# Scores of 64 rows in the two row halves of TensorE: time mixing head by head, sparse attention two parities at a time

## The chip, the cores and the metric

One core of one Trainium2 chip. The metric is the device time of one launch in microseconds (us), the median of several runs. The engines are PE (TensorE), with its weight loads shown apart as PEld, DVE (VectorE), ACT (ScalarE), POOL (GpSimd) and SP (SyncE, which issues DMAs). PSUM has eight banks of 128 x 512 in f32.

## What is computed

Two transformer blocks after one another on a row of 256 tokens of 1024 values, in f32. Each has two mixers and two feed-forward layers. The change is in three of the mixers: RWKV time mixing, differential attention and sparse attention. Cut to what matters:

```python
# time mixing, 16 heads of 64: a state S per head, token by token
sa = einsum('bhvk,bhk->bhv', S, a)
S = S * w[:, :, None, :] + sa[..., None] * b[:, :, None, :] + v[..., None] * k[:, :, None, :]
y = einsum('bhvk,bhk->bhv', S, r)
...
# differential attention, 8 heads with two scores (c) of 64 each
s = einsum('bqhcd,bkhcd->bhcqk', qb, k)
p = softmax(where(mask, s, -inf))
a = p[:, :, 0] - lam * p[:, :, 1]
...
# sparse attention: 64 keys of each query chosen by 8 index heads, then 16 heads of 64
dots = einsum('bqhe,bke->bqhk', qib, k_idx)
score = einsum('bqh,bqhk->bqk', wb, relu(dots))
vals, idx = top_k(where(mask, score, -inf), topk)
s = einsum('bqhd,bqkhd->bhqk', qb, gather(k, idx))
```

## The kernel before

The stages run in the order time mixing, ffn, latent attention, ffn, differential attention, mlp, sparse attention, mlp. Tokens are two blocks (b) of 128. The large products take three matmuls each, of high and low parts of both sides (L284, L285, L286, 128 x 512 per matmul or 128 x 256); L88 on ACT and L89 on DVE or POOL cut each weight tile into its parts when it has come by DMA.

A stage puts its latency-bound steps (generators) and the large products (a list `bg`, stepped by `tick`) into one program order; `weave` steps the generators in turn, `attention` runs `part1` (scores, softmax) of each item and `part2` (transposed rows times V) `lag` items later, with so many ticks behind each. The final order on each engine is not this one: the tile framework's scheduler sets it from priorities (attention's steps carry one) and its own timeline. On the chip each engine then runs its row in that order, and waits by semaphores.

The scores have 64 rows to contract. Features lie two heads to a tile of 128 partitions, so head s of a pair is the half 64s to 64s + 63. In the attentions a head's score is a matmul of K = 64 in one half (L1137, L1287 for the index heads, L1311). In time mixing `rwkv_scores` takes both heads of a pair in one matmul of K = 128: its right side is a tile of 256 columns in which each head's 128 columns have zeros in the other head's rows (L1820, two pairs to a bank, then the mask L1822 on DVE and a yield; twice per call). It is called 16 times: by block and half of the features (H) for the system matrix (`rwkv_strict`), V's part (`rwkv_solve`), and two reads (`rwkv_reads`). After the first of these come, in time mixing:

- L1717: 32 x 32 blocks of the system on PE, their mask L1719, splits L1725 to L1729, and a transpose L1728;
- L1735 to L1746: forward substitution on DVE, 14 rounds of a product (L1740) and a sum (L1741), closed by L1744 to L1746;
- `rwkv_merge`: L1763, L1770, L1783, L1796, small products of 16 and 32 columns on PE with DVE steps between, for each half;
- `rwkv_solve` (L1835, L1838, L1846, L1851) and `rwkv_out` (L1935, L1938, L1942), matmuls of 64 columns.

PSUM is split in rings by kind: time mixing takes its scores from a ring `tp` of four banks (four more are for products or longer sums, by part), the attentions from one of three. `turns` gives the SBUF rooms that `take` hands out: e for softmax rows, n and o for smaller ones, r for the relu rows of `select`, which finds the 64 keys by eight rounds of DVE (L1302, L1303).

Of the kernel before, what the change touches and what calls it, by code (L numbers as in the profile page):

```python
# [15 lines left out]
AF = mybir.ActivationFunctionType  # L16
# [3 lines left out]
T = 256  # L20
# [9 lines left out]
class Feeder:  # L30
    """Weights in the order of their use: DMA ahead, then cut into two float32r parts, in tiles that go round."""
# [14 lines left out]
    def grow(self, n):  # L46
        """Slots for n more units cut ahead; those that are too many go as they get free."""
# [53 lines left out]
    def put(self, unit):  # L101
        """The unit has had its last use."""
        self._give(unit[2])
# [33 lines left out]
def first(f):  # L137
    """The method's instructions go before others that are ready, those of block 0 before those of block 1."""
# [10 lines left out]
class K:  # L149
# [20 lines left out]
    def turns(self, **n):  # L170
        """Slots for one kind of tile each, taken in turn, till the next call."""
# [11 lines left out]
    def rings(self, acc=4, tp=4, long=0, po=0):  # L183
        """The banks of PSUM in rings: products, short-lived, longer-lived, halves for attention's sums."""
# [17 lines left out]
    def sm(self, n, tag=None, bufs=None):  # L202
        """A few columns, taken in turn from as many as there are of that kind."""
# [9 lines left out]
    def wide(self, key, n, bufs):  # L213
        """The same for wider ones."""
# [7 lines left out]
    def bcast(self, vec, n, q=None):  # L222
        """A row of DRAM on every partition, in a slot."""
# [17 lines left out]
    def sumsq(self, parts, n):  # L241
        """Mean of squares of the rows over n columns, from the parts of a row; [128, len(parts)]."""
# [9 lines left out]
    def rstd(self, ss, eps=EPS):  # L252
        """(sum of the columns of ss + eps) ** -0.5"""
# [9 lines left out]
    def transpose_split(self, src, hi, lo, b, kts):  # L263
        """Token-major columns of src (128 each) to feature-major parts of block b."""
# [27 lines left out]
    def gemm_b_steps(self, nkt, widths, lhs, done, rk=2, tail=0, head=0, before_b1=None):  # L292
        """Token-major products: for each column piece, acc[b][128 tokens, width]; yields after each weight unit."""
# [51 lines left out]
    def gemm_b1(self, nkt, nh, lhs, done, rk=2):  # L345
        """Token-major products, all columns of block 0 before block 1: the weights are kept between."""
# [33 lines left out]
    def weave(self, gens, every=1, n=1):  # L380
        """One step of each in turn; n steps of the products behind them after every so many turns."""
# [24 lines left out]
    def pre_norm(self, b, g):  # L406
        """x * rstd * g of block b, token-major."""
# [15 lines left out]
    def norm_in(self, g):  # L423
        """The normed rows of both blocks, feature-major, before the weights that had to wait."""
# [6 lines left out]
    class PostNorm:  # L431
        """x += m * rstd(m) * g, the columns of m arriving in halves."""
# [18 lines left out]
    class Add:  # L451
        """x += m"""
# [10 lines left out]
    def load_rows_t(self, pieces, name):  # L463
        """Rows of 128 values (a vector cut in rows, several vectors under one another) as columns."""
# [24 lines left out]
    def gemm_a(self, hi, lo):  # L489
        """Feature-major product: two tiles of 128 features, 256 tokens."""  # L490
# [14 lines left out]
    def gemm_a_first(self, hi, lo):  # L505
        """Two such products, of the blocks one after the other: token-major, then turned."""
# [118 lines left out]
    def rope_setup(self):  # L625
        """cos and sin of [token, block, frequency]: 16 of the first block's, 8 of the second's."""
# [40 lines left out]
    def rope_pair(self, x1, x2, cos1, sin1, cos2, sin2, room=None):  # L667
        """x1, x2 <- x1 cos1 - x2 sin1, x2 cos2 + x1 sin2 (all [128, heads, half])."""
# [1374 lines left out]
```

## Time and profile before

| | us |
|---|---|
| median of 3 runs | 1434.3 |
| lowest and highest | 1432.52 and 1442.06 |
| profiled execution, span | 1429.5 |
| PE busy | 1351.8 |
| DVE busy | 937.9 |
| ACT busy | 705.4 |

The profiled execution is shown by its span, from the first to the last instruction; the time of a run has a few us around it. A matmul in f32 is two records of PE in the trace, one in the cut parts. An entry such as 64*128 64x256 says that the tile mode is 64 rows by 128 columns of the array and that 64 partitions with 256 columns move. PE pipelines, so the time from one start to the next says what a matmul takes of it, and its length is longer.

### The profile page before, as it was taken

The numbers are of one execution on the slowest core, as the hardware profiler recorded it, in microseconds if no ns is written. First come the engines' busy times: TensorE is split into PE (matmuls) and PEld (weight loads), VectorE is DVE, ScalarE is ACT, GpSimd is POOL, SyncE is SP. The second block draws the span as 40 slices with busy tenths as digits, with TensorE's granted clock in tenths as the row PEclk, the third lists the DMA queues.
The fourth block names the chain that finished last, engine by engine and source line by source line (L and its number), as shares of the span: only waits on it lengthen the run. The fifth ranks groups of instructions, "written<-read, shape, count | busy, mean of one in ns | idle before, by whom it ended". The sixth has DMA issues, their size and how long they took to land. (4 is left out here: it accounts for less than half of the span.)

```text
span 1429.5 us, 22837 instructions
## 1 busy us (share of the span) xinstructions
PE 1351.8 (95%) x8907; PEld 1178.2 (82%) x8907; DVE 937.9 (66%) x1526; ACT 705.4 (49%) x1168; POOL 370.7 (26%) x300
## 2 busy tenths in 40 slices
PE   7978799999999899999999999999999998999998
PEld 5667699799988787799987777699888777799987
DVE  7899755777654775767644788667433896576542
ACT  5753222565543665565553555455443546465431
POOL 6545841200000100132232353222322531111110
PEclk9989699999999999999999999999999999999999
DMA  7323301475573452366574543266663642266562
GB/s 245 118 88 120 102 4 61 161 228 185 184 235 99 148 166 59 96 218 192 187 213 135 177 148 118 89 197 202 210 192 97 206 121 72 74 193 191 191 193 88
DMA packets 153420, 214.39 MB, mean 150 GB/s; under 512 B 11668, under 2 KB 95868, under 8 KB 153312
## 3 DMA queue, kind: packets, MB, share of 16 engines
q1 hardware_dynamic: 152448, 209.78, 47.1%
q10 hardware_dynamic: 864, 3.15, 0.6%
q8 instruction: 70, 1.15, 0.3%
q14 instruction: 38, 0.31, 0.1%
HBM read 211.85 MB, written 1.05 MB: 149 GB/s over the span
## 5 line engine op out<-in xcount | busy, mean ns | idle before, releaser
L88 ACT ACTIVATE s_slot<-s_slot 128x1024 fp32r<-128x1024 f32 (+2 forms) x221 | 229.4, 1048 | 178.4 <-PE bank L286 95.1
L89 DVE TENSOR_TENSOR s_slot<-s_slot,s_slot 128x1024 fp32r<-128x1024 f32 (+3 forms) x172 | 221.5, 1296 | 132.2 <-ACT s_slot L88 130.8
L89 DVE TENSOR_TENSOR rwkv_slot<-s_slot,rwkv_slot 128x1024 fp32r<-128x1024 f32 (+4 forms) x121 | 157.4, 1309 | 119.1 <-ACT rwkv_slot L88 118.7
L89 POOL TENSOR_TENSOR s_slot<-s_slot,s_slot 128x1024 fp32r<-128x1024 f32 x49 | 119.3, 2437 | 310.3 <-ACT s_slot L88 295.7
L88 ACT ACTIVATE rwkv_slot<-s_slot 128x1024 fp32r<-128x1024 f32 (+3 forms) x141 | 144.2, 1035 | 106.2 <-PE bank L286 64.1
L260 POOL TENSOR_TENSOR rwkv_sm<-rwkv_sm,mhalf 128x1 f32<-128x1 f32 x32 | 20.0, 625 | 338.0 <-DVE rwkv_sm L257 337.2
L284 PE MATMUL bank<-ffn_slot,s_slot 128*128 128x256 f32 x320 | 90.8, 284 | 2.4 <-DVE ffn_slot L539 2.4
L285 PE MATMUL bank<-ffn_slot,s_slot 128*128 128x256 f32 x320 | 90.6, 283 | 0.0
L286 PE MATMUL bank<-ffn_slot,s_slot 128*128 128x256 f32 x320 | 90.6, 283 | 0.0
L284 PE MATMUL bank<-ffn_slot,rwkv_slot 128*128 128x256 f32 x280 | 79.4, 284 | 0.0
L285 PE MATMUL bank<-ffn_slot,rwkv_slot 128*128 128x256 f32 x280 | 79.3, 283 | 0.0
L286 PE MATMUL bank<-ffn_slot,rwkv_slot 128*128 128x256 f32 x280 | 79.2, 283 | 0.0
L284 PE MATMUL bank<-mlp_slot,s_slot 128*128 128x256 f32 x272 | 77.0, 283 | 0.0
L286 PE MATMUL bank<-mlp_slot,s_slot 128*128 128x256 f32 x272 | 77.0, 283 | 0.0
L285 PE MATMUL bank<-mlp_slot,s_slot 128*128 128x256 f32 x272 | 77.0, 283 | 0.0
L89 POOL TENSOR_TENSOR rwkv_slot<-s_slot,rwkv_slot 128x1024 fp32r<-128x1024 f32 (+1 forms) x20 | 48.3, 2413 | 93.6 <-ACT rwkv_slot L88 89.6
L284 PEld LDWEIGHTS bank<-ffn_slot,s_slot 128*128 128x128 f32 x320 | 61.4, 192 | 2.8 <-ACT rwkv_slot L88 1.4
L284 PE MATMUL bank<-s_slot,mlp_slot 128*128 128x512 f32 x160 | 62.6, 391 | 0.4 <-ACT mlp_slot L274 0.3
L286 PE MATMUL bank<-s_slot,mlp_slot 128*128 128x512 f32 x160 | 62.6, 391 | 0.0
L285 PE MATMUL bank<-s_slot,mlp_slot 128*128 128x512 f32 x160 | 62.3, 389 | 0.0
L286 PEld LDWEIGHTS bank<-ffn_slot,s_slot 128*128 128x128 f32 x320 | 61.4, 192 | 0.0
L285 PEld LDWEIGHTS bank<-ffn_slot,s_slot 128*128 128x128 f32 x320 | 61.4, 192 | 0.0
(516 smaller groups left out, 3917.7 us busy)
## 6 DMA issues: line engine op xcount, KB each, us to landing
s_slot<-in_mlp_w_dram SPq DMA_DIRECT2D x128, 512.0 KB
s_slot<-in_ffn_w_in_dram SPq DMA_DIRECT2D x88, 512.0 KB
s_slot<-in_ffn_w_out_dram SPq DMA_DIRECT2D x44, 512.0 KB
s_slot<-in_a_w_rkv_dram SPq DMA_DIRECT2D x24, 512.0 KB
s_slot<-in_diff_w_in_dram SPq DMA_DIRECT2D x32, 256.0 KB
s_slot<-in_dsa_w_in_dram SPq DMA_DIRECT2D x16, 512.0 KB
s_slot<-in_a_w_o_dram SPq DMA_DIRECT2D x8, 512.0 KB
s_slot<-in_o_w_dram SPq DMA_DIRECT2D x8, 512.0 KB
```

The lines of the kernel that those rows point to most:

```text
L88: k.nc.scalar.activation(hi, raw, AF.Copy)
L89: (k.nc.gpsimd if low else k.nc.vector).tensor_tensor(lo, raw, hi, op=OP.subtract)
L260: nc.gpsimd.tensor_tensor(r, u, self.mhalf[:, 0:1], op=OP.pow)
L284: mm(out, lh, rh, start=start, stop=False)
L285: mm(out, lh, rl, start=False, stop=False)
L286: mm(out, ll, rh, start=False, stop=stop)
```

## The change

Four places. `rwkv_scores` takes two banks, one for each row half, and makes one matmul of K = 64 per head, alternating between the halves; the masks follow per bank (a strided view of S), with one yield. Differential attention takes its two banks first and alternates between them. `select` does the same with its two halves, and takes its relu rooms from e. `attend` gets tuples of parities: sparse attention takes both parities of a group in one item, with a lag of 1 instead of 3, ticks [4, 2, 2, 2] instead of [2, 1, 1, 1] and rooms e = 6 without r; latent attention keeps one parity per item. Lines behind these move: L1717 is L1727, L1735 to L1741 are L1745 to L1751, L1746 is L1756, L1820 is L1832, L1822 is L1834, L1835 is L1847, L1851 is L1863, L1935 is L1947, L1942 is L1954, L1311 is L1321.

```diff
-    def attend(self, score, V, scale, sel, out, ready, ticks, lag, order):
+    def attend(self, score, V, scale, sel, out, ready, ticks, lag, order, both):
...
-            pr = (4 * g + s, 4 * g + 2 + s)
-            ps = self.tp()
-            for i, hd in enumerate(pr):
-                score(hd, b, ps[:, i * 256:i * 256 + nk], nk)
-            e = self.take("e", 2, 2, 256)
+            ps = [self.tp() for _ in ss]
             for i in range(2):
+                for s, p in zip(ss, ps):
+                    score(4 * g + 2 * i + s, b, p[:, i * 256:i * 256 + nk], nk)
+            es = [self.take("e", 2, 2, 256) for _ in ss]
...
-        self.attention([[(*i, s) for i in items for s in range(2)] for items in self.items(order)], part1, part2, ready, ticks, lag)
+        parts = [(0, 1)] if both else [(0,), (1,)]
+        self.attention([[(*i, ss) for i in items for ss in parts] for items in self.items(order)], part1, part2, ready,
+                       ticks, lag)
...
-            for c in range(2):
-                ps = self.tp()
-                for i in range(2):
+            pss = [self.tp() for _ in range(2)]
+            for i in range(2):
+                for c, ps in enumerate(pss):
                     nc.tensor.matmul(ps[:, i * 256:i * 256 + nk], QK.head(g, 2 * i + c, b * 128, b * 128 + 128),
                                      QK.head(g, 4 + 2 * i + c, 0, nk), start=True, stop=True)
+            for c, ps in enumerate(pss):
...
-        self.turns(e=5, n=4, o=2, r=2)
+        self.turns(e=6, n=4, o=2)
...
-            for j, (i, s) in enumerate(((0, 0), (0, 1), (1, 0), (1, 1))):
-                ps = self.tp()
-                rows = slice(64 * s, 64 * s + 64)
-                rl = self.take("r", 2, 256)
+            for i in range(2):
+                pss = [self.tp() for _ in range(2)]
                 for m in range(2):
-                    nc.tensor.matmul(ps[:, m * 256:m * 256 + nk], IQ[rows, 2 * i + m, b * 128:(b + 1) * 128],
-                                     IK[rows, 0, :nk], start=True, stop=True)
...
+                    for s, ps in enumerate(pss):
+                        rows = slice(64 * s, 64 * s + 64)
+                        nc.tensor.matmul(ps[:, m * 256:m * 256 + nk], IQ[rows, 2 * i + m, b * 128:(b + 1) * 128],
+                                         IK[rows, 0, :nk], start=True, stop=True)
+                rls = [self.take("e", 2, 256) for _ in range(2)]
...
-                    ready, [2,1,1,1], 3, 1)
+                    ready, [4,2,2,2], 1, 1, True)
...
         S = self.slot([128, 8, 128])
-        for j in range(2):
-            p = self.tp()
-            for i in range(2):
-                nc.tensor.matmul(p[:, 256 * i:256 * i + 256], F[:, 2 * j + i, tok], rhs[:, 2 * j + i], start=True,
-                                 stop=True)
-            nc.vector.tensor_tensor(S[:, 4 * j:4 * j + 4], p.rearrange("p (m t) -> p m t", m=4),
+        Sv = S.rearrange("p (f s) t -> p s f t", s=2)
+        ps = [self.tp() for _ in range(2)]
+        for f in range(4):
+            for s, p in enumerate(ps):
+                r = slice(64 * s, 64 * s + 64)
+                nc.tensor.matmul(p[:, 128 * f:128 * f + 128], F[r, f, tok], rhs[r, f, s], start=True, stop=True)
+        for s, p in enumerate(ps):
+            nc.vector.tensor_tensor(Sv[:, s], p.rearrange("p (m t) -> p m t", m=4),
                                     self.over_heads(self.tri[kind], 4), op=OP.mult)
-            yield
+        yield
         return S
```

The order of the instructions moves with it. On PE in the late part of time mixing, before (L1820 the scores, L1935 the reads times V; banks 67 to 70 are the scores'):

```order
L1820 MATMUL bank_67<-rwkv_slot_1565,rwkv_slot_622 128x256
L1820 MATMUL bank_68<-rwkv_slot_1574,rwkv_slot_635 128x256
L1820 MATMUL bank_69<-rwkv_slot_1530,rwkv_slot_725 128x256
L1820 MATMUL bank_70<-rwkv_slot_1540,rwkv_slot_736 128x256
L1820 MATMUL bank_68<-rwkv_slot_1574,rwkv_slot_635 128x256
L1820 MATMUL bank_69<-rwkv_slot_1530,rwkv_slot_725 128x256
L1820 MATMUL bank_67<-rwkv_slot_1565,rwkv_slot_622 128x256
L1935 MATMUL bank_71<-rwkv_slot_325,rwkv_slot_1751 128x64
L1935 MATMUL bank_72<-rwkv_slot_326,rwkv_slot_1759 128x64
L1935 MATMUL bank_71<-rwkv_slot_325,rwkv_slot_1751 128x64
```

The same place after (L1832 the scores, one head each, each bank with one half; L1947 the former L1935):

```order
L1832 MATMUL bank_69<-rwkv_slot_1560,rwkv_slot_725 128x128
L1832 MATMUL bank_67<-rwkv_slot_1618,rwkv_slot_635 128x128
L1832 MATMUL bank_68<-rwkv_slot_1570,rwkv_slot_635 128x128
L1947 MATMUL bank_71<-rwkv_slot_325,rwkv_slot_1782 128x64
L1832 MATMUL bank_70<-rwkv_slot_1609,rwkv_slot_622 128x128
L1832 MATMUL bank_69<-rwkv_slot_1560,rwkv_slot_725 128x128
L1947 MATMUL bank_71<-rwkv_slot_325,rwkv_slot_1782 128x64
L1832 MATMUL bank_67<-rwkv_slot_1618,rwkv_slot_635 128x128
L1832 MATMUL bank_70<-rwkv_slot_1609,rwkv_slot_622 128x128
L1947 MATMUL bank_71<-rwkv_slot_325,rwkv_slot_1782 128x64
L1832 MATMUL bank_68<-rwkv_slot_1570,rwkv_slot_635 128x128
L1832 MATMUL bank_67<-rwkv_slot_1618,rwkv_slot_635 128x128
```

Scores that stood in a row of eight now stand one to three at a time between calls of 64 columns.

On DVE at the head of the forward substitution, before (L1725, L1726, L1728 make its operand, L1822 are masks of scores, L1735 and L1740 its first steps):

```order
L1725 TENSOR_SCALAR rwkv_slot_786<-rwkv_slot_783,even_odd 128x32x16
L1822 TENSOR_TENSOR rwkv_slot_843<-bank_71,rwkv_slot_266 128x512
L1726 SCALAR_TENSOR_TENSOR rwkv_slot_786<-rwkv_slot_783,even_odd,rwkv_slot_786 128x32x16
L1728 STREAM_TRANSPOSE rwkv_slot_785<-rwkv_slot_786 128x512
L1822 TENSOR_TENSOR rwkv_slot_931<-bank_72,rwkv_slot_266 128x512
L1822 TENSOR_TENSOR rwkv_slot_935<-bank_73,rwkv_slot_266 128x512
L1735 COPY rwkv_slot_785<-rwkv_slot_785 128x2
L1822 TENSOR_TENSOR rwkv_slot_931<-bank_74,rwkv_slot_266 128x512
L1822 TENSOR_TENSOR rwkv_slot_935<-bank_71,rwkv_slot_266 128x512
L1740 TENSOR_TENSOR rwkv_slot_787<-rwkv_slot_785 128x2x4
```

The same place after (L1735, L1736, L1738 make the operand, L1834 are the masks, L1745 and L1750 the first steps):

```order
L1739 TENSOR_SCALAR rwkv_slot_784<-rwkv_slot_783,even_odd 128x32x16
L1834 TENSOR_TENSOR rwkv_slot_919<-bank_72,rwkv_slot_266 128x4x128
L1834 TENSOR_TENSOR rwkv_slot_930<-bank_74,rwkv_slot_266 128x4x128
L1735 TENSOR_SCALAR rwkv_slot_786<-rwkv_slot_783,even_odd 128x32x16
L1834 TENSOR_TENSOR rwkv_slot_930<-bank_71,rwkv_slot_266 128x4x128
L1834 TENSOR_TENSOR rwkv_slot_919<-bank_73,rwkv_slot_266 128x4x128
L1736 SCALAR_TENSOR_TENSOR rwkv_slot_786<-rwkv_slot_783,even_odd,rwkv_slot_786 128x32x16
L1738 STREAM_TRANSPOSE rwkv_slot_785<-rwkv_slot_786 128x512
L1745 COPY rwkv_slot_785<-rwkv_slot_785 128x2
L1750 TENSOR_TENSOR rwkv_slot_787<-rwkv_slot_785 128x2x4
```

The masks of the same four banks of scores (slots 931 and 935 before, 919 and 930 after) stand behind L1728 before, and ahead of L1736 after.

On PE, the scores for which these masks wait, after (bank_72 and bank_74, bank_71 and bank_73 are the masks' banks in turn; L284 to L286 large products):

```order
L286 MATMUL bank_69<-s_slot_85,rwkv_slot_863 128x512
L1832 MATMUL bank_71<-rwkv_slot_204,rwkv_slot_736 128x128
L284 MATMUL bank_69<-s_slot_85,rwkv_slot_861 128x512
L285 MATMUL bank_69<-s_slot_86,rwkv_slot_861 128x512
L1832 MATMUL bank_71<-rwkv_slot_204,rwkv_slot_736 128x128
L286 MATMUL bank_69<-s_slot_85,rwkv_slot_863 128x512
L284 MATMUL bank_70<-s_slot_85,rwkv_slot_861 128x512
L1832 MATMUL bank_74<-rwkv_slot_204,rwkv_slot_736 128x128
L1832 MATMUL bank_72<-rwkv_slot_192,rwkv_slot_725 128x128
L1832 MATMUL bank_71<-rwkv_slot_204,rwkv_slot_736 128x128
L285 MATMUL bank_70<-s_slot_86,rwkv_slot_861 128x512
L1832 MATMUL bank_73<-rwkv_slot_192,rwkv_slot_725 128x128
```

Before, these scores (L1820 on banks 71 to 74) were two rows of calls with products between the rows; after, the last ones stand singly between products.

## Rows read from the trace of the kernel before

**Rows 1.** Part 1 of the page: busy time, share of the span and instructions of each engine.

```profile
PE 1351.8 (95%) x8907; PEld 1178.2 (82%) x8907; DVE 937.9 (66%) x1526; ACT 705.4 (49%) x1168; POOL 370.7 (26%) x300
```

**Rows 2.** Table by stretches; columns: length, busy PE, PEld, DVE, ACT, POOL, PEclk, DMA share, GB/s.

```profile
105.00:143.00 38.00, 32.90 (x268) 26.95 (x266) 35.00 (x54) 15.59 (x20) 18.57 (x10) 0.96 0.40 125
143.00:182.00 39.00, 31.40 (x827) 26.39 (x828) 29.18 (x32) 10.37 (x16) 32.52 (x19) 0.64 0.31 93
182.00:245.00 63.00, 62.77 (x562) 58.86 (x561) 31.00 (x58) 10.49 (x19) 15.82 (x37) 1.00 0.08 26
...
1165.00:1200.00 35.00, 29.71 (x144) 22.50 (x142) 30.23 (x100) 19.34 (x52) 10.43 (x8) 0.90 0.30 91
```

**Rows 3.** Timeline of PE, the merge; columns: start, length, engine, line, operation, idle before.

```profile
148.05 1.22 PE L1820 MATMUL bank<-rwkv_slot,rwkv_slot 128*128 128x256 f32 x2
...
153.04 2.37 PE L1770 MATMUL bank<-rwkv_slot,rwkv_slot 32*32 32x16 f32 x204
...
185.64 1.89 PE L1820 MATMUL bank<-rwkv_slot,rwkv_slot 128*128 128x256 f32 x8
187.47 0.73 PE L1851 MATMUL bank<-rwkv_slot,rwkv_slot 64*64 64x64 f32 x9
```

**Rows 4.** Timeline of PE: a burst in both halves, and a burst in one.

```profile
1141.23 1.13 PE L1287 MATMUL bank<-dsa_slot,dsa_slot 64*128 64x256 f32 x8
1142.29 0.50 PE L286 MATMUL bank<-s_slot,dsa_slot 128*128 128x512 f32 x1
...
878.50 0.40 PE L286 MATMUL bank<-rwkv_slot,diff_slot 128*128 128x512 f32 x1
878.83 1.13 PE L1137 MATMUL bank<-diff_slot 64*128 64x256 f32 x4
879.88 0.50 PE L284 MATMUL bank<-rwkv_slot,diff_slot 128*128 128x512 f32 x1
880.22 0.39 PE L285 MATMUL bank<-rwkv_slot,diff_slot 128*128 128x512 f32 x1
```

**Rows 5.** Timeline of PE: single calls in one half between transposes.

```profile
861.98 0.48 PE L1137 MATMUL bank<-diff_slot 64*128 64x128 f32 x2
862.39 0.33 PE L268 MATMUL bank<-ident,diff_slot 128*128 128x128 f32 x1
862.65 0.48 PE L1137 MATMUL bank<-diff_slot 64*128 64x128 f32 x2
```

**Rows 6.** Waits of PE, 143 to 182 us: total, times, longest.

```profile
PE bank L1763 <- DVE rwkv_slot L1744: 5.1, 1, 5.1
PE bank L1770 <- issue: 3.0, 1, 3.0
```

**Rows 7.** Timeline of PE and DVE around the forward substitution.

```profile
107.85 2.06 PE L1717 MATMUL bank<-rwkv_slot,rwkv_slot 128*32 128x64 f32 x128
...
115.99 1.12 DVE L1726 SCALAR_TENSOR_TENSOR rwkv_slot<-rwkv_slot,even_odd,rwkv_slot 128x512 f32<-128x512 f32 x1
...
120.22 0.15 DVE L1740 TENSOR_TENSOR rwkv_slot<-rwkv_slot 128x8 f32<-128x8 f32 x1
...
121.69 2.04 DVE L1740 TENSOR_TENSOR rwkv_slot<-rwkv_slot 128x50 f32<-128x50 f32 x1
...
124.07 2.29 DVE L1740 TENSOR_TENSOR rwkv_slot<-rwkv_slot 128x72 f32<-128x72 f32 x1
...
143.44 0.71 DVE L1746 STREAM_TRANSPOSE rwkv_slot<-rwkv_slot 128x512 f32<-128x512 f32 x1
```

**Rows 8.** Timeline of POOL and ACT in the same stretch.

```profile
121.25 2.40 POOL L89 TENSOR_TENSOR s_slot<-s_slot,s_slot 128x1024 fp32r<-128x1024 f32 x1 [2.19 <-issue]
...
122.73 1.06 ACT L88 ACTIVATE s_slot<-s_slot 128x1024 fp32r<-128x1024 f32 x1 [1.61 <-PE bank L286]
```

**Rows 9.** Sparse attention's scores, grouped (min/median/max ns, first and last start), and PE's wait.

```profile
L1311 PE MATMUL bank<-dsa_slot,dsa_slot x64: 272/374/480, 1164.6 to 1225.9; 64*128 64x128 f32 x32, 64*128 64x256 f32 x32
...
1185.64 0.69 PE L717 MATMUL bank<-ident,dsa_slot 128*128 128x128 f32 x2 [1.68 <-DVE dsa_slot L1054]
```

More of the change, by code (lines that the diff above doesn't have):

```diff
@@ L773, in part1, with part2 @@
         def part1(it):
-            g, b, s = it
+            g, b, ss = it
             nk = 128 * (b + 1)
-            if s == 0:
+            if ss[0] == 0:
                 po[g, b], sums[g, b] = self.bank("po"), self.sm(4, tag="sums", bufs=4)
-            pr = (4 * g + s, 4 * g + 2 + s)
-            ps = self.tp()
-            for i, hd in enumerate(pr):
-                score(hd, b, ps[:, i * 256:i * 256 + nk], nk)
-            e = self.take("e", 2, 2, 256)
-            self.soft_rows(ps, nk, scale, sel and sel[b], [sums[g, b][:, hd % 4:hd % 4 + 1] for hd in pr], e[:, 0], e[:, 1])
-            return e
-        def part2(it, e):
-            g, b, s = it
-            t = self.p_transpose([e[:, 0, 0], e[:, 0, 1]], b + 1, e[:, 1])
-            for i in range(2):
-                hd = 4 * g + 2 * i + s
-                for kb in range(b + 1):
-                    nc.tensor.matmul(po[g, b][:, hd % 4 * 64:hd % 4 * 64 + 64], t[:, i, kb, :], V(kb, hd), start=kb == 0,
-                                     stop=kb == b)
-            if s == 0:
+            ps = [self.tp() for _ in ss]
+            for i in range(2):
+                for s, p in zip(ss, ps):
+                    score(4 * g + 2 * i + s, b, p[:, i * 256:i * 256 + nk], nk)
+            es = [self.take("e", 2, 2, 256) for _ in ss]
+            for s, p, e in zip(ss, ps, es):
+                self.soft_rows(p, nk, scale, sel and sel[b], [sums[g, b][:, 2 * i + s:2 * i + s + 1] for i in range(2)],
+                               e[:, 0], e[:, 1])
+            return es
+        def part2(it, es):
+            g, b, ss = it
+            for s, e in zip(ss, es):
+                t = self.p_transpose([e[:, 0, 0], e[:, 0, 1]], b + 1, e[:, 1])
+                for i in range(2):
+                    hd = 4 * g + 2 * i + s
+                    for kb in range(b + 1):
+                        nc.tensor.matmul(po[g, b][:, hd % 4 * 64:hd % 4 * 64 + 64], t[:, i, kb, :], V(kb, hd),
+                                         start=kb == 0, stop=kb == b)
+            if ss[-1] == 0:
                 return None
@@ L1281, in select @@
             sc, wk, md = box[:, 0, :nk], box[:, 1, :nk], box[:, 2, :nk]
[L1282 to L1285 removed]
+            for i in range(2):
+                pss = [self.tp() for _ in range(2)]
                 for m in range(2):
[L1287 to L1296 removed]
+                    for s, ps in enumerate(pss):
[3 more added lines that the diff above has]
+                rls = [self.take("e", 2, 256) for _ in range(2)]
+                for ps, rl in zip(pss, rls):
+                    nc.scalar.activation(rl[:, :, :nk], ps.rearrange("p (m k) -> p m k", m=2)[:, :, :nk], AF.Relu)
+                for s, rl in enumerate(rls):
+                    for m in range(2):
+                        hd = 2 * (2 * i + m) + s
+                        w = wi[b][:, hd:hd + 1]
+                        if i == s == m == 0:
+                            nc.vector.tensor_scalar(sc, rl[:, 0, :nk], w, None, op0=OP.mult)
+                        else:
+                            nc.vector.scalar_tensor_tensor(sc, rl[:, m, :nk], w, sc, op0=OP.mult, op1=OP.add)
                 yield
```

10 lines of the change are left out of this document (1 added, 9 removed).

## Prediction

> **What bounds the kernel now.** I read the page's busy shares first: PE is busy for 95% of the span, so it is the engine to look at [rows 1]. Then the table by stretches [rows 2]: from 182 to 245 us PE has 62.77 us of work in 63, so what is added to PE there or taken away moves the end one for one. From 105 to 143 it has 32.90 of 38, from 143 to 182 31.40 of 39 at a clock of 0.64: there a chain on DVE and the short products that follow it hold the time. From 1165 to 1200 DVE's search for the 64 largest scores and PE share the time (30.23 and 29.71 of 35). In the feed-forward stages nothing is changed but, here and there, the order of products; I take ±1 us for them.
>
> The profiled span is 1429.5 us, the median of the runs 1434.3; the 4.8 us between lie around the program, and I take them as constant. The runs lie 9.5 us apart, so about 1% (14 us) is what a measurement can tell from no change.
>
> **Prices.** Each matmul in f32 is two records. From the starts on PE: eight records of L1820 (128 x 256) take 187.47 - 185.64 = 1.83 us, the change of mode behind them in it [rows 3], so 0.216 each for those inside the row; one of 64 x 256 has as many columns and is taken alike, one of 64 x 128 at half, 0.11 (two of them and the step out of them are 0.41 [rows 5]). Two bursts in different row halves with different banks do run side by side where they stand next to each other: 8 records of L1287 (four of 128 columns in one half, four of 256 in the other) take from their start to the next 1142.29 - 1141.23 = 1.06 us, and four of 64 x 256 alone 879.88 - 878.83 = 1.05 [rows 4]. So the halves are worth what the change says, if the order lets them meet.
>
> What a burst in row halves costs beside its records is in the same stretches: the first record after the change of mode comes 0.33 us after an f32r product that takes 0.23 otherwise, and the product behind it 0.34 [rows 4]. With 4 x 0.216 = 0.86 of work in the 1.05, one trip into the halves and out costs 0.10 + 0.19 + 0.11 = 0.40 us. Between transposes of one record, 861.98 to 862.65 is one round with three records of 0.11 in 0.67 us: 0.34 per trip [rows 5]. A lone head there pays 0.34 for 0.22 of work. Each change of mode shows in each of these rows, so I count every one.
>
> The Trainium skill's page "TensorEngine Tiling (Array Packing)", section "Key Properties", says that changing the tiling mode, and not only the tile, drains TensorE. The rows agree (0.34 to 0.40 a trip), and the page gives no price. Its section "Theoretical Speedup" promises up to two times for 64 rows; by that the scores would take half as long, which is rival (c).
>
> **The change part by part.**
>
> *Time mixing, late part (from 187 us on).* Here PE is full. Before, the scores are K = 128 calls in the same mode as the products around them, in rows of eight; in the order after, single heads alternate with single calls of L1947, the former L1935. Counted over the whole order from the first L1851 to the first L1942: 9 changes of mode before, 61 after, so 26 trips more. At 0.34 that is +8.8 us (at 0.29, if part of the first record's delay is hidden, 7.5; at 0.40, 10.4). Against it the work: 72 records of 0.216 before are 15.6 us; after, 80 heads are 160 records of 0.112, 17.9 us one after the other, and 13.1 with those halves side by side that the order puts next to each other: -2.5 us. Sum **+6.3 us**, from +5 to +8. The masks stay 32 of the same size.
>
> *Time mixing, early part (107 to 187 us).* Three things. First PE's work: 56 records of 0.216 (12.1 us) become 48 heads in 10.8 us one by one, or 6.2 as the order pairs them; the changes of mode go from 10 to 24, 7 trips or 2.4 to 2.8 us. So PE does some 3 us less, in a stretch in which it waited 5.1 us for L1744 and 3.0 within the merge anyway [rows 6].
>
> Second, DVE's queue. The forward substitution (L1740 and L1741, 14 rounds) starts at 120.22 and its last transpose at 143.44 [rows 7]. In the order after, the four masks of the second scores stand ahead of L1736 and L1738, which feed the chain's head (before: behind L1728). The first of them, of bank_72, waits for a single head that stands on PE behind two bursts of heads, 15 + 5 products of L284 to L286 and three other singles. From the start of L1717 (107.85 [rows 7], L1727 after): 2.2 us for L1727, 4.8 for 26 heads in three visits, 20 products at 0.23 with 0.34 for the first of a row, 5.0, and 4 singles at 0.34 + 0.22 with some of them paired, 1.7: about 121.5, where DVE with its four earlier masks would be ready at about 115. Behind it come the other three masks, L1735, L1736, L1738 and L1745; now the same steps without the first splitting one (0.5) take 120.22 - 115.99 = 4.2 us [rows 7], so the chain's first round would start at about 126, **some 6 us later**. Queued behind are all rounds of the chain, and PE's L1763 waits for its end. Against that, rounds of L1740 last 2.04 and 2.29 us where the first takes 0.15 [rows 7], beside an L89 on POOL of 2.40 us [rows 8]; each L89 follows an L88 on ACT that waits for PE's L286 [rows 8], not for the chain, so one or two would be done before the late head begins. That gives back 1.9 to 3.9 us, and a third such round may follow; I take 3.5, so the chain ends about 3 us later.
>
> Third, the merge (143 to 187 us) after the chain. Before, PE puts L1820 and products between L1763, L1770, L1783, L1796 and L1851: 5.0 us from 148.05 to 153.04, and again before L1851 begins at 187.47 [rows 3]. After, 8 heads and 5 products of these stand ahead of the merge. Part of them is cover for the waits (PE idles 3.0 for L1770 beside them [rows 6]); the first filler alone is 5.0 us, and if that much was in the way, the end of the merge comes 5 us sooner, from 2 to 8. Sum for the early part **-2 us**, from -6 to +7.
>
> *Sparse attention.* The 32 calls of L1311 are 32 records of 0.112 and 32 of 0.216, 10.5 us [rows 9]. Two banks stand next to each other in one place before and in four after, three of them in different halves: 10.05 us of work becomes 8.74, and three trips go, at 0.40: -2.5. In the selection the order splits the pairs that met before (1141.23 is one [rows 4]): 5 bursts become 7 and 3.90 us 4.58, +1.5 in a full stretch. Relu rooms from the ring of e, a lag of one instead of three items: no instruction more. PE waits there 1.68 us for L1054 at 1185.64 [rows 9]; with twice the ticks behind each item it may wait less or DVE's chain may come later: ±4. Sum **-1 us**, from -5 to +4.
>
> *Differential attention.* 13 bursts before and after, with the same work of 8.74 us: the pairs that the code writes were made by the order already, and those that it did not make it doesn't make now. **0**, ±1.5. The latent attention keeps one half at a time: 0.
>
> Sum: 6.3 - 2 - 1 = +3.3 us, a span of 1432.8 and, with the 4.8 around it, **1437 us**.
>
> **The rivals.** (a) *The merge gains more than the changes of mode cost.* If all 8 us between the merge's steps go while the chain's head is only 2 late, and sparse attention gets its 5: 5 - 6 - 5 = -6, 1428 us. For it speaks that PE's idle time sits just there [rows 6]; against it that the cover is still needed at L1770 and L1783. (b) *Slower: DVE's queue at the chain's head.* If the L89 on POOL still fall on the chain's first rounds, the head's 6 us arrive whole at L1763; the fewer products between the steps then only turn into idle time, and the late part pays 0.40 a trip: 6 + 8 = +14, 1448 us. It decides from the point where fewer than two of the L89 are done before the first long round. For it: 14 rounds in one queue, nothing else hides them, and PE's longest wait of the stretch is for them [rows 6]. Against: PE has less work before the chain, so the head's score is made sooner. (c) *The halves meet everywhere.* Sixteen calls of rwkv_scores at 8 x 0.112 + 0.40 = 1.3 us are 20.7 instead of 27.6; sparse attention with 8 bursts instead of 15 saves 7 trips and as many half bursts, some 7 us; differential attention 5 trips and bursts, 5; selection 1.5: -20, 1414 us. The Trainium skill's "up to 2x" (same page, "Theoretical Speedup") would come to about this. Against it stands the order itself, in which single heads are spread among other products. (d) *PE hides the trips*, because the records of the next mode's weights are loaded ahead: then 26 trips cost nothing, -2.5 - 2 - 1 = -5.5, 1429 us. Rows 5 speak against it, where each single pays.
>
> **How the numbers follow.** The forecast with its own spread (1432 to 1442) has a chance of 0.52, (a) 0.14, (d) 0.10, (b) 0.18, (c) 0.06. The range leaves out (c) and the far half of (b) and reaches 3 us below (a) for the ±1 and ±1.5 of the stages taken at nothing: 1425 to 1448. Faster by over 1% (below 1420) is (c) and little else: 0.06. Slower by over 1% (above 1448.6) is not quite half of (b), with the stages taken at nothing on top: 0.08. The rest, 0.86, is within 1%.
>
> **What would show it.** In the profile after: from the first L1863 to the first L1954 5 to 8 us more than from L1851 to L1942 before, with PE still full, records of L1832 alone between L1947, and 0.2 us into and out of each; the first L1750 at 125 to 128, not 120; the last DVE transpose of the chain (L1756) 2 to 5 us later, but the first L1863 at or before 187. In sparse attention, fewer and longer bursts and the same end of top-k. The forecast is wrong if the trips among 128 x 64 products cost less than 0.2 us, if the chain's end moves by the full 6 us, or if the share of waits from 1165 to 1200 changes by more than 4 us.

## The result and the profile after

The changed kernel takes 1489.16 us (median of 4 runs, 1482.97 to 1493.89) where the one before took 1435.5 beside it: a ratio of 1.0375, with an interval from 1.0351 to 1.0398. Forecast were 1437 us and a range up to 1448; it is some 53 us slower. The profiled execution, the fastest of the four, has a span of 1481.1 us, 51.6 more than before.

The page's busy line and its row of granted clocks, after (each digit a fortieth of the span; 9 is full speed, 5 half):

```profile
PE 1388.3 (94%) x9035; PEld 1208.6 (82%) x9035; DVE 939.1 (63%) x1526; ACT 704.6 (48%) x1168; POOL 372.6 (25%) x300
...
PEclk9989676699999999999999999999999998999999
```

The row of granted clocks before:

```profile
PEclk9989699999999999999999999999999999999999
```

PE has 36.5 us more work than before [rows 1], though the records of time mixing's scores add up to about the same (256 of 0.11 us where 128 of 0.22 were). Four slices in a row, from 148 to 296 us, stand at 6 or 7; before, one did, that of the merge. The table by stretches, after (columns as in [rows 2]: length, busy PE, PEld, DVE, ACT, POOL, granted clock, DMA share, GB/s):

```profile
105.00:143.00 38.00, 36.01 (x317) 28.26 (x315) 29.00 (x39) 15.33 (x21) 24.38 (x12) 1.00 0.39 120
143.00:182.00 39.00, 23.92 (x767) 20.44 (x769) 31.71 (x42) 10.80 (x17) 26.62 (x15) 0.61 0.30 99
...
182.00:190.00 8.00, 7.28 (x127) 6.96 (x121) 5.23 (x7) 2.38 (x5) 7.87 (x6) 1.00 0.01 2
190.00:212.00 22.00, 21.66 (x134) 19.47 (x133) 6.46 (x21) 2.50 (x5) 4.78 (x30) 0.53 0.00 1
212.00:235.00 23.00, 22.77 (x197) 19.99 (x196) 9.90 (x17) 1.18 (x2) 0.00 (x0) 1.00 0.07 25
235.00:283.00 48.00, 48.00 (x238) 44.12 (x239) 12.91 (x20) 5.07 (x8) 3.83 (x4) 0.50 0.06 23
283.00:290.00 7.00, 7.00 (x46) 6.27 (x45) 4.94 (x6) 3.37 (x5) 0.00 (x0) 0.99 0.70 234
```

Before, the stretch from 182 to 245 us stood at 1.00 with PE full [rows 2]. Now PE is as full, 48.00 of 48 from 235 to 283, but 22 us stand at 0.53 and 48 at 0.50: the lower of TensorE's two levels, 1.2 GHz where 2.4 were granted before. Start to start of PE, after: where the clock fell, a round of heads and reads at full clock, and the same at half:

```profile
188.25 2.08 PE L1863 MATMUL bank<-rwkv_slot,rwkv_slot 64*64 64x64 f32 x32 [0.68 <-ACT rwkv_slot L1860]
190.25 2.50 PE L1832 MATMUL bank<-rwkv_slot,rwkv_slot 64*128 64x128 f32 x16
192.68 0.58 PE L1858 MATMUL bank<-rwkv_slot,rwkv_slot 64*64 64x64 f32 x3
...
224.93 0.49 PE L1832 MATMUL bank<-rwkv_slot,rwkv_slot 64*128 64x128 f32 x4
225.35 0.43 PE L1947 MATMUL bank<-rwkv_slot,rwkv_slot 128*128 128x64 f32 x2
225.71 0.49 PE L1832 MATMUL bank<-rwkv_slot,rwkv_slot 64*128 64x128 f32 x4
...
240.84 0.79 PE L1832 MATMUL bank<-rwkv_slot,rwkv_slot 64*128 64x128 f32 x2
241.56 0.69 PE L1947 MATMUL bank<-rwkv_slot,rwkv_slot 128*128 128x64 f32 x2
242.18 0.80 PE L1832 MATMUL bank<-rwkv_slot,rwkv_slot 64*128 64x128 f32 x4
```

From 224.93 to 225.71 two heads in both halves and one read take 0.78 us, 0.44 of it their records (two of 0.11 for the pair, two for the read), so the trip is 0.34, as forecast. From 240.84 to 242.18, at half clock, one head and one read take 1.34. The last thing before the first fall, at about 191, were a wait of 0.68 us, 64 x 64 products (L1863, to 190.25) and the 16 records in row halves; it came back at about 211, in the 128 x 128 products of L1871 and L1872, and fell again at 235 behind singles (L1832 and L1947 in turns from 223.6) and L1863.

Where the 51.6 us arose, by the starts of the same calls in both traces: the first L1863 (L1851) comes 0.8 later, the first L1954 (L1942) 37.5, the first scores of latent attention (L988, before L982) 40.6, the first scores of differential attention 44.3, the first index scores of sparse attention 42.8, and the end 51.6. So time mixing's late part has 36.7 of it, the stretch behind it, at half clock to 283 us, another 3, and what follows 11, most of it from sparse attention on.

At the head of the substitution, DVE and POOL after:

```profile
121.75 1.29 DVE L1834 TENSOR_TENSOR rwkv_slot<-bank,rwkv_slot 128x512 f32<-128x512 f32 x2 [6.80 <-PE bank L1832]
...
126.72 1.91 DVE L1745 COPY rwkv_slot<-rwkv_slot 128x2 f32<-128x2 f32 x1
128.73 0.17 DVE L1750 TENSOR_TENSOR rwkv_slot<-rwkv_slot 128x8 f32<-128x8 f32 x1
...
130.22 2.06 DVE L1750 TENSOR_TENSOR rwkv_slot<-rwkv_slot 128x50 f32<-128x50 f32 x1
132.62 2.01 DVE L1750 TENSOR_TENSOR rwkv_slot<-rwkv_slot 128x72 f32<-128x72 f32 x1
...
129.81 7.09 POOL L89 TENSOR_TENSOR s_slot<-s_slot,s_slot 128x1024 fp32r<-128x1024 f32 x3
...
151.39 0.71 DVE L1756 STREAM_TRANSPOSE rwkv_slot<-rwkv_slot 128x512 f32<-128x512 f32 x1
```

The mask of bank_72 and its neighbour start at 121.75 after 6.80 us of waiting for PE's L1832: the forecast had 121.5, and DVE ready at 115. The first round starts at 128.73, 8.5 us later than before [rows 7], and the last transpose at 151.39, 8.0 later. Two L89 on POOL were done before the head, as the forecast said, but others stood behind them (three in a row from 129.81), so the long rounds are still stretched to 2.06 and 2.01 us. PE's longest waits of the stretch, after:

```profile
PE bank L1773 <- DVE rwkv_slot L1754: 9.3, 1, 9.3
...
PE bank L1780 <- issue: 1.6, 1, 1.6
```

PE waits 9.3 us for the chain where it waited 5.1 [rows 6]; the merge behind it is 7.2 us shorter than before (151.39 to 188.25, and 143.44 to 187.47 [rows 3, 7]) and takes the delay back.

### The profile page after: what moved, and what is told of

Its sections match the earlier page's. It is cut to its first block, busy times and chain, and to the rows that moved or that the text cites. A ratio compares the mean times of both kernels' runs of the same rounds, so it can differ in the third digit from the quotient of the medians.

```text
span 1481.1 us, 23076 instructions
## 1 busy us (share of the span) xinstructions
PE 1388.3 (94%) x9035; PEld 1208.6 (82%) x9035; DVE 939.1 (63%) x1526; ACT 704.6 (48%) x1168; POOL 372.6 (25%) x300
## 5 line engine op out<-in xcount | busy, mean ns | idle before, releaser
L89 DVE TENSOR_TENSOR s_slot<-s_slot,s_slot 128x1024 fp32r<-128x1024 f32 (+3 forms) x172 | 223.8, 1309 | 131.2 <-ACT s_slot L88 130.4
L89 DVE TENSOR_TENSOR rwkv_slot<-s_slot,rwkv_slot 128x1024 fp32r<-128x1024 f32 (+4 forms) x121 | 159.4, 1324 | 119.4 <-ACT rwkv_slot L88 119.0
L89 POOL TENSOR_TENSOR s_slot<-s_slot,s_slot 128x1024 fp32r<-128x1024 f32 x49 | 121.5, 2483 | 331.7 <-ACT s_slot L88 326.1
L284 PE MATMUL bank<-ffn_slot,s_slot 128*128 128x256 f32 x320 | 91.4, 286 | 3.9 <-DVE ffn_slot L539 3.9
L286 PE MATMUL bank<-ffn_slot,s_slot 128*128 128x256 f32 x320 | 91.1, 285 | 0.0
L284 PE MATMUL bank<-ffn_slot,rwkv_slot 128*128 128x256 f32 x280 | 79.4, 284 | 0.0
L286 PE MATMUL bank<-ffn_slot,rwkv_slot 128*128 128x256 f32 x280 | 79.2, 283 | 0.0
L284 PE MATMUL bank<-mlp_slot,s_slot 128*128 128x256 f32 x272 | 77.0, 283 | 0.0
L286 PE MATMUL bank<-mlp_slot,s_slot 128*128 128x256 f32 x272 | 77.0, 283 | 0.0
L89 POOL TENSOR_TENSOR rwkv_slot<-s_slot,rwkv_slot 128x1024 fp32r<-128x1024 f32 (+1 forms) x20 | 48.2, 2410 | 96.7 <-ACT rwkv_slot L88 92.0
L284 PEld LDWEIGHTS bank<-ffn_slot,s_slot 128*128 128x128 f32 x320 | 62.1, 194 | 4.2 <-issue 2.8
L284 PE MATMUL bank<-s_slot,mlp_slot 128*128 128x512 f32 x160 | 62.6, 391 | 0.4 <-ACT mlp_slot L274 0.3
L286 PE MATMUL bank<-s_slot,mlp_slot 128*128 128x512 f32 x160 | 62.6, 391 | 0.0
L286 PEld LDWEIGHTS bank<-ffn_slot,s_slot 128*128 128x128 f32 x320 | 62.1, 194 | 0.0
```

The source lines that it names most:

```text
L89: (k.nc.gpsimd if low else k.nc.vector).tensor_tensor(lo, raw, hi, op=OP.subtract)
L284: mm(out, lh, rh, start=start, stop=False)
L286: mm(out, ll, rh, start=False, stop=stop)
```

## The experiments

Thirteen more kernels ran. The late part, the changes of mode and the clock in the table are those of one traced execution: the late part goes from the first L1851 (its Y matmul) to the first L1942 (its last read), by whatever line these have there; the changes of tile mode in it are counted in the order. The run is the median of all runs; e2, e5, e8 and e12 ran once. The trace is of the fastest run for the changed kernel, e1 and e3, and of the slowest for e4, e7 and e13.

| kernel | late part, us | changes of mode | granted clock there | run, us | before beside it |
|---|---|---|---|---|---|
| before | 53.2 | 9 | 1.00 | 1435.5 | |
| changed kernel | 89.9 | 61 | 0.5 and 1.0 | 1489.16 | 1435.5 |
| e1, old time mixing | 53.2 | 9 | 1.00 | 1442.66 | 1437.34 |
| e2, time mixing only | 91.7 | 61 | 0.5 and 1.0 | 1476.59 | 1437.34 |
| e3, full rows | 56.7 | 21 | 1.00 | 1462.29 | 1437.34 |
| e4, grouped | 65.4 | 43 | 0.5, then 1.0 | 1456.63 | 1437.34 |
| e5, full rows and added modes | 146.2 | 140 | mostly 0.5 | 1557.9 | 1436.24 |
| e6, early calls only | 53.0 | 9 | 1.00 | 1440.55 | 1436.24 |
| e7, late calls grouped | 85.2 | 42 | mostly 0.5 | 1473.17 (1448.84 once) | 1436.24 |
| e8, late calls as written | 102.6 | 66 | mostly 0.5 | 1482.75 | 1436.24 |
| e12, fewer scores | 67.5 | 13 | 1.0, then 0.5 | 1451.62 | 1430.1 |
| e13, work added | 86.7 | 69 | mostly 1.0 | 1486.51 | 1434.43 |

**Which part costs (e1, e2).** e1 puts the old `rwkv_scores` into the changed kernel, e2 the new one into the kernel before:

```diff
-        Sv = S.rearrange("p (f s) t -> p s f t", s=2)
-        ps = [self.tp() for _ in range(2)]
-        for f in range(4):
-            for s, p in enumerate(ps):
...
+        for j in range(2):
+            p = self.tp()
+            for i in range(2):
+                nc.tensor.matmul(p[:, 256 * i:256 * i + 256], F[:, 2 * j + i, tok], rhs[:, 2 * j + i], start=True,
+                                 stop=True)
```

> The changed kernel with time mixing's scores as before (K = 128, two heads to a matmul); the three attention parts of the change stay. Theory: of the +53 us, about 43 are made in time mixing, where the granted clock shows 0.50 for some 68 us in the late part; the trace after shows +4 more before differential attention's scores and +6 in sparse attention. So this run gives about 1435 + 10 = 1445 us, with 1.00 in the late part of time mixing. Rival: the attentions' delays only follow from time mixing (other arrival of weights), then 1435. Rival: the attentions themselves cost most, then above 1465.

> The kernel before with the new scores of time mixing alone. Theory: the late part falls to 0.50 as in the changed kernel, 1435 + 43 = 1478 us. Rival (the attentions cost it): under 1445.

e1 gave a ratio of 1.0042 (1.0019 to 1.0065), 6 us: the three attention parts together. e2, one run, stands 39 us above the runs of before, with the half clock of the changed kernel. So some 40 of the 53 us are in `rwkv_scores`, and the clock falls without the attentions' part of the change. Some 8 us show in neither alone; the runs of the changed kernel lie 11 apart.

**Row halves or single calls (e3).** Only the rows of the same calls change:

```diff
                 r = slice(64 * s, 64 * s + 64)
-                nc.tensor.matmul(p[:, 128 * f:128 * f + 128], F[r, f, tok], rhs[r, f, s], start=True, stop=True)
+                nc.tensor.matmul(p[:, 128 * f:128 * f + 128], F[:, f, tok], rhs[:, f, s], start=True, stop=True)
```

> The changed kernel, but each head of time mixing's scores contracts all 128 rows (the other head's 64 are zeros in the right side), so it is the same single matmul of 128 columns in nearly the same order, without the row halves: 21 changes of mode in the late part, not 61. Theory (the row halves with their changes of mode bring the clock down): 1.00 in the late part, scores 80 x 0.224 us instead of 36 x 0.432, +2.4, and 6 more trips than before, +2: about 1450 us with the attentions' 10. Rival (single scores among calls of 64 columns bring it down, whatever their rows): 0.50 as in the changed kernel and 1485.

Windows of e3, columns as above:

```profile
182.00:190.00 8.00, 7.28 (x126) 6.96 (x118) 3.92 (x7) 2.04 (x4) 8.00 (x4) 1.00 0.01 2
...
200.00:220.00 20.00, 19.35 (x175) 19.12 (x174) 6.51 (x13) 1.18 (x2) 0.00 (x0) 1.00 0.07 27
220.00:240.00 20.00, 20.00 (x211) 19.10 (x210) 8.87 (x15) 1.78 (x3) 0.00 (x0) 1.00 0.01 2
240.00:260.00 20.00, 18.77 (x132) 16.83 (x132) 10.11 (x14) 5.71 (x8) 3.83 (x4) 1.00 0.17 57
260.00:280.00 20.00, 16.34 (x64) 12.90 (x63) 16.13 (x29) 8.87 (x16) 4.86 (x6) 0.83 0.48 159
```

In this trace the clock stays at 1.00 through the late part, which takes 56.7 us: single heads between calls of 64 columns, contracting 128 rows, don't bring it down here. PE's wait ahead of the late part is the changed kernel's (7.28 us of work in 8 from 182 to 190 us in both), so that wait by itself doesn't either. But the trace is of the fastest of four runs, 1453.58 us at a mean granted clock of 0.967; the others took 1460.66, 1463.92 and 1471.37 at 0.964, 0.960 and 0.953, and where their clock was lower no trace shows. The whole is slower than expected, 1.0196 (1.0154 to 1.0239): in the traced run, beside the attentions' 6 us, some 7 more are lost behind the late part, between 250 and 280 us, where PE waits 3.0 us for L1968 and the clock falls (0.83 from 260 to 280). Why these calls come late there I didn't settle.

**Fewer changes of mode (e4).**

```diff
+        with self.tc.high_priority(1000):
+            for f in range(4):
+                for s, p in enumerate(ps):
...
```

> The changed kernel with the eight heads of a call at a high priority, so that they stand in runs of four and more: 43 changes of mode in the late part, not 61, the same half rows. If the number of changes brings the clock down, part of the fall goes: 1455 to 1470 us. If the half rows do, whatever their order, 0.50 stays and it is 1480 to 1490. If only the lone singles do, 1.00 comes back: about 1445.

```profile
200.00:220.00 20.00, 20.00 (x120) 18.51 (x119) 5.70 (x19) 2.95 (x5) 0.00 (x0) 0.51 0.01 1
220.00:240.00 20.00, 20.00 (x178) 18.28 (x177) 10.20 (x17) 0.59 (x1) 0.00 (x0) 1.00 0.08 28
```

1.0139 (1.0108 to 1.017): two thirds of the loss are back. The clock is at 0.50 for nearly all of the late part up to 219 us, among 64 x 64 products and half-row runs of eight, comes back in L1872 and L1873 (the 128 x 128 products) and then holds 1.00 through the other runs, with PE full. So half rows and changes of mode, as few as here, don't force the fall wherever they stand.

**Early calls, late calls (e6, e7, e8).** In the kernel before, e6 takes the new heads for the system matrix only, e8 for all other calls, and e7 the same as e8 in e4's grouped form:

```diff
-            E["SM", b] = yield from self.rwkv_scores(E, b, E["A2"][b], 0, 0)
+            E["SM", b] = yield from self.rwkv_half(E, b, E["A2"][b], 0, 0)
...
```

> The kernel before with half-row heads for the system matrix alone (the first four calls), all other scores and the attentions as before. Theory: the substitution starts 8 us later and the merge takes that back, as in the changed kernel, where the first L1863 came 0.7 later than L1851 before; the late part stays at 1.00: 1437 us, within 4. Rival: the half rows early bring the clock down for what follows, over 1445.

> The kernel before with the half-row heads as the change writes them in all calls but the system matrix: the substitution and the merge are as before, the late part has singles (66 changes of mode). Theory: 0.50 for most of the late part, 1470 us. Rival (the later substitution, or the idle time of PE before the merge, opened the fall): 1.00 and 1440.

> The kernel before with half-row heads at a high priority (runs of four to sixteen) in all calls but the system matrix, which stays at K = 128, so that the late part is entered as before. 42 changes of mode in the late part, not 9: 16 trips of 0.36, +6, and -2.5 for the paired records. Theory (spread singles take too much full-row work out of a stretch; runs beside dense calls don't): 1.00 stays, 1440 us. Rival (half rows bring the clock down in any order): 0.50 in the late part, over 1455.

e6: 1.0025 (1.0008 to 1.0041), with the first round at 129.1 and the first L1851 at 191.2: the chain's head costs some 4 us (1 to 6), and the clock is at 1.00 in the late part. e8, one run, which leaves the chain where it was (first round at 119.7), falls like the changed kernel; windows of e8:

```profile
200.00:220.00 20.00, 19.23 (x123) 17.63 (x121) 8.41 (x23) 1.08 (x3) 0.00 (x0) 0.76 0.00 1
220.00:240.00 20.00, 20.00 (x107) 17.02 (x106) 4.54 (x7) 0.59 (x1) 0.00 (x0) 0.50 0.09 26
240.00:260.00 20.00, 20.00 (x114) 16.68 (x113) 3.87 (x6) 1.18 (x2) 0.00 (x0) 0.50 0.00 1
```

The later substitution is not what opens the fall. e7 came out otherwise than expected: its four runs are 1448.84 once, at a mean granted clock of 0.966, and 1473.0 to 1477.93 three times, at 0.945 to 0.950, and the trace, of the slowest, shows mostly half clock. One run was near the 1440 expected; grouping doesn't hold the clock reliably, and what set that run apart no trace shows.

**What brings the clock down (e5, e12, e13).** e5 keeps the full-row heads of e3 and adds small half-row matmuls, whose result is overwritten:

```diff
-                nc.tensor.matmul(p[:, 128 * f:128 * f + 128], F[r, f, tok], rhs[r, f, s], start=True, stop=True)
+                if m or kind:
+                    nc.tensor.matmul(p[:, 128 * f:128 * f + 32], F[r, f, tok], rhs[r, f, s, :32], start=True, stop=True)
+                nc.tensor.matmul(p[:, 128 * f:128 * f + 128], F[:, f, tok], rhs[:, f, s], start=True, stop=True)
```

> The full-row heads of the run before, and ahead of each head outside the system matrix a small matmul of 64 rows and 32 columns into the same place, which the head then overwrites: it adds changes of mode (140 in the late part, not 21) and next to no work in half rows, and takes no full-row work away. If the changes of mode alone bring the clock down: 0.50 through the late part, which then takes 140 us or more. If it is the full-row work that the half rows take away: 1.00, and the late part takes its 57 us there, 60 trips of 0.34 and 80 small calls of 0.1 more, about 85 us.

```profile
200.00:220.00 20.00, 20.00 (x100) 17.44 (x100) 4.44 (x16) 2.42 (x5) 0.52 (x17) 0.50 0.00 1
...
240.00:260.00 20.00, 20.00 (x83) 18.51 (x84) 0.69 (x1) 0.59 (x1) 0.00 (x0) 0.50 0.07 27
```

Mostly 0.50, 146.2 us, all of them with PE busy: changes of mode are enough, with all the full-row work there and no idle time. But they also stretch the time over which that work lies. e12 therefore takes dense work out of the kernel before and adds nearly no change of mode (the late calls' function against the former one):

```diff
-            for i in range(2):
-                nc.tensor.matmul(p[:, 256 * i:256 * i + 256], F[:, 2 * j + i, tok], rhs[:, 2 * j + i], start=True,
-                                 stop=True)
+            nc.tensor.matmul(p[:, :128], F[:, 2 * j, tok], rhs[:, 2 * j, 0], start=True, stop=True)
...
```

> The kernel before with most of the late scores left out: outside the system matrix one matmul of K = 128 and 128 columns stands for two of 256, and its mask reads that one head for all four, so the time mixing's result is not computed. The change of mode stays rare (13 in the late part, 9 before), but 18 calls of 0.22 us are left of 36 of 0.43, as the half rows too take dense work away. If the changes of mode are needed for the clock to fall: 1.00, the late part takes 53.2 - 11.6 + 0.7, about 42 us, and the run 1425. If less dense work in the stretch is enough: 0.50 for much of it, the late part 60 to 85 us and the run 1445 to 1470.

```profile
190.00:200.00 10.00, 8.90 (x103) 8.39 (x100) 6.74 (x22) 2.95 (x5) 4.38 (x27) 1.00 0.01 2
200.00:220.00 20.00, 20.00 (x108) 19.76 (x106) 7.66 (x14) 1.18 (x2) 0.00 (x0) 0.53 0.08 27
220.00:240.00 20.00, 20.00 (x130) 19.06 (x130) 4.59 (x8) 2.27 (x4) 0.00 (x0) 0.50 0.06 15
240.00:260.00 20.00, 20.00 (x97) 20.00 (x96) 6.46 (x10) 1.13 (x3) 4.09 (x4) 0.50 0.09 38
```

The clock falls at about 201 us and is at 0.50 to the end of the late part, which takes 67.5 us; the run, the only one, stands 21.5 us above the one of before: less work, more time. What opened the fall here may be the 1.1 us that PE waited from 190 to 200 (e3 waited 0.65 from 200 to 220 and kept 1.00); but for 50 us after that PE is full and the clock doesn't come back. Many changes of mode are not needed for that. The 128 x 128 products, in which it came back in the changed kernel, stand ahead of the fall here (193 to 197 us); it comes back at about 266, in the large products L284 to L286. Most of PE's work from 240 to 260 is reads of 64 columns (L1949, L1952, L1956). The kernel before makes such reads too (L1935, L1938), with PE as full, at 1.00:

```profile
235.00:240.00 5.00, 5.00 (x48) 5.00 (x46) 3.19 (x6) 0.00 (x0) 4.09 (x4) 1.00 0.50 195
```

So the same calls run on at either level, and a fall here lasted until other work came.

e13 goes the other way, from the changed kernel:

```diff
+        if m or kind:
+            for p in ps:
+                for f in range(2):
+                    nc.tensor.matmul(p[:, 256 * (f % 2):256 * (f % 2) + 256], F[:, f, tok], rhs[:, f], start=True, stop=True)
```

> The changed kernel with work added: outside the system matrix each call of the scores first makes four matmuls of K = 128 and 256 columns into its banks, which the heads then overwrite. The row halves and their changes of mode stay (69 in the late part, 61 in the changed kernel); the added matmuls are 40 of 0.43 us there, 17 us at full clock. If the share of dense work in the stretch holds the clock: 1.00 comes back in most of the late part, 31 us saved against 17 added, 1470 to 1480, faster than the changed kernel with more work. If the changes of mode bring it down whatever stands beside them: 0.50 stays, and 17 to 34 us come on top, 1505 to 1525.

```profile
200.00:220.00 20.00, 19.13 (x135) 16.57 (x134) 7.25 (x19) 1.08 (x3) 0.00 (x0) 0.91 0.00 1
220.00:240.00 20.00, 20.00 (x121) 16.97 (x119) 3.18 (x5) 0.59 (x1) 0.00 (x0) 0.78 0.07 27
240.00:260.00 20.00, 20.00 (x174) 16.96 (x173) 5.24 (x8) 1.18 (x2) 0.00 (x0) 0.88 0.00 1
```

With 17 us of matmuls more and eight more changes of mode the late part is 3.2 us shorter, 86.7, in a trace of its slowest run, since the clock is now above 0.75 in each of these windows. In whole, 1.0357 (1.0335 to 1.0379) is no different from the changed kernel, and above the 1470 to 1480 expected: the clock came back for most of the late part, not all, and time is lost behind it (the first scores of latent attention come 49.4 us later than before, in the changed kernel 40.6). It still fell near 231 us, behind half-row heads and L1951 in turns from 228.2 on, without an added matmul between them.

**The attentions (e9, e10, e11).** Each alone in the kernel before, by the diff of the change (e9 with its own relu rooms, e10 with relu rows in the rooms e):

> The kernel before with only the selection's index scores in the new order (relu rooms still their own). Theory: the pairs that met are split, 95 changes of mode in the program instead of 91, +1.5 us and, since DVE's top-k starts later, up to 3 us: 1437 to 1439. Rival: nothing to be seen, 1436.

> The kernel before with only sparse attention's items of both parities (lag 1, ticks 4, 2, 2, 2, six rooms e that the relu rows share). Theory: 87 changes of mode instead of 91 save 2.5 us of PE, but with the time mixing's scores as before the changed kernel lost 6 us between 1155 and 1232 us, where PE waits 2.8 for L1060 before the first scores and the clock is 0.66 from 1185 to 1205; that comes from here: 1440 us. Rival (it comes from the selection): 1434.

> The kernel before with only differential attention's two banks taken first. 91 changes of mode as before. Theory: no difference, 1436 us within 2. Rival (the written pairs meet after all): 1431.

e11: 0.9992 (0.9978 to 1.0007), nothing. e9: 1.0062 (1.0032 to 1.0093). e10: 1.0072 (1.0049 to 1.0095). Either change in sparse attention costs 9 or 10 us alone, both together (e1) 6; the intervals overlap. Windows of e9, of e10, and of the kernel before:

```profile
1165.00:1185.00 20.00, 15.76 (x76) 11.53 (x75) 19.97 (x67) 9.31 (x20) 6.48 (x6) 1.00 0.45 144
1185.00:1205.00 20.00, 13.22 (x58) 10.83 (x57) 13.53 (x37) 8.07 (x25) 4.26 (x3) 0.63 0.18 55
```

```profile
1165.00:1185.00 20.00, 15.14 (x59) 11.41 (x58) 20.00 (x64) 4.82 (x8) 11.14 (x9) 0.83 0.40 131
1185.00:1205.00 20.00, 12.56 (x53) 9.58 (x51) 13.18 (x34) 10.17 (x26) 4.75 (x2) 0.74 0.32 106
```

```profile
1185.00:1205.00 20.00, 18.28 (x95) 15.03 (x96) 12.95 (x43) 9.68 (x33) 4.00 (x2) 0.84 0.16 53
```

DVE is full to 1185 us as before, and PE then has 13.22 and 12.56 us of work in 20, at 0.63 and 0.74; before it has 18.28 there at 0.84. PE waits for DVE steps (L1050 for L1039 3.8 us in e9, L284 for L1038 4.7 in e10), and the clock falls beside that. Which instruction's new place starts this was not tried.

## Why the prediction was wrong

**The step that failed** is the sum of the late part, "+6.3 us, from +5 to +8", which measured +36.7. The terms that it has held: the trip is 0.34, the count of 61 came about, and by an estimate from the windows, if 22 us at 0.53 and the 43 us at 0.50 up to 278.1 had run at 1.00 (10.3 and 21.5 us less), 58.1 us would be left, +4.9. What it lacked is the clock: trips and halves were priced with rows at 1.00, and the table of stretches showed 1.00 for the whole late part [rows 2], which I took as given. The changed kernel (0.53 and 0.50) against e1 (1.00, 53.2 us) shows that it depends on how the scores are made; e3 (1.00, 56.7 us) agrees in the one run that a trace shows. No rival had it.

**Why the clock fell.** Before, the heads' zeros were part of calls of 128 rows by 256 columns, 36 of them between products of 64 columns and 64 x 64 blocks. In e12 most of their dense work is gone, without row halves, and the clock falls and stays down with PE full. In e5 the changes of mode bring it down with that work kept, and in e13 dense work put beside the changes of mode brings much of it back. All three fit one account: ahead of the falls PE did less dense full-row work in the stretch than before, since it was halved or left out or lay among trips. That this is the cause is argued and not shown: e5 stretches and thins at once, so the trips may act in another way too, e12 has a wait ahead of its fall, and both ran once. Idle time of PE doesn't divide the kernels: e5 fell and stayed down in a late part without any, e3 kept 1.00 with 0.65 us of it from 200 to 220. The Trainium skill ("TensorE: Matmul & The Clock Gate", "HAM oscillation — how this bites in real kernels") puts such a fall down to idle gaps of PE. The trace here differs: it fell at 235 us with PE busy for 22.77 of the 23 us before, and stayed at 0.50 with 48.00 of 48 busy, where the profile counts the trips as busy.

**The early part**, -2 forecast, was +0.8. The mask's wait came as worked out (121.75 for 121.5), the chain's head at 128.7 for 126, as a copy at 126.72 lasted 1.91 us beside POOL's L89 (0.15 before, at 118.96 us, with no L89 beside it). The give-back of 3.5 by earlier L89 failed: further ones took their place, and the chain's end moved by 8.0, past the full 6 that the prediction names as a sign of being wrong. The merge gave back 7.2 for the 5 forecast. The 4.8 us that the forecast adds around the span are not there either: span and time of the later runs lie 1.9 apart (1481.1 and 1482.97).

**Sparse attention**, -1 with up to +4, was the other mis-sized term: e1 shows +6 for all the attentions, e9 and e10 +9 and +10 alone. PE's shorter scores brought nothing in a stretch in which DVE is full (to 1185 us), and the new order left PE waiting. **Differential attention**, 0, is right (e11).

**The rivals.** (b) had the place of the late head but the wrong size of its price: 8.5 us at the head, some 4 at the end (e6). (a) had the merge right, and nothing else. (c), the halves meeting everywhere, didn't come about: 128 more records than before with most bursts alone. (d) fell by the trips' 0.34.

No version here beats the kernel before; the best of them is differential attention's part alone, no different from it.

## What to carry to other kernels

Before work is taken off PE in a stretch of small matmuls, look at what holds its clock there: the padded, wasteful calls may be what does, and a stretch that is full at 1.00 can be just as full at 0.50. Two row halves ran side by side only where they stood next to each other (eight records in 1.06 us [rows 4]), and no kernel here was faster by them; count the changes of tile mode in the final order, at 0.34 to 0.40 us a trip here, and price the stretch at half clock as a rival. A scheduler that breaks up the pairs, as here, takes the gain and leaves the cost.

## What the runs showed of the hardware

Leaving out scores made a run slower (e12: 1451.62 us beside 1430.1), and adding 17 us of matmuls shortened a stretch by 3.2 (e13), both by the granted clock. Reads of 64 columns with PE full ran at 1.00 in the kernel before (235 to 240 us) and at 0.50 in e12 (240 to 260). The same program can differ from run to run in it: e7 took 1448.84 us once, at a mean of 0.966, and 1473.0 to 1477.93 three times, at 0.945 to 0.950. A copy of 128 x 2 on DVE took 1.91 us beside an L89 on POOL, and 0.15 before without one.
